# A chained down projection: order of low halves and sums in its first chunk, order and PSUM tiles in its last

## The chip, the cores and the metric

The kernel runs on one core of one Trainium2 chip. The metric is the device time of one execution in microseconds (us), lower is better. The core has a matrix engine (TensorE, PE in the profile), three engines for elementwise work (VectorE or DVE, ScalarE or ACT, GpSimd or POOL), a sync engine (SP) that issues DMAs, an on-chip memory (SBUF) of 128 partitions, and a small accumulator memory (PSUM) into which the matrix engine writes.

## The reference

One decoder layer on 1024 tokens of width 1024 in float32: norm, two gated branches, output projection and residual, then an MLP and a last norm. The change lies in the MLP's second product and the last norm:

```python
    h = rms_norm(x, g_mlp[l])
    f = jnp.square(jax.nn.relu(jnp.einsum("bsd,df->bsf", h, w_1[l])))
    x = x + jnp.einsum("bsf,fd->bsd", f, w_2[l])
return rms_norm(x, g_final)
```

Here f has 4096 columns, w_2 is 4096 x 1024, and rms_norm divides each token's row by the root of its mean square (plus 1e-6) and multiplies it by a gain per column. All of it is float32.

## The kernel before

**The down projection** (f times w_2) is the last stage. The 4096 rows of the sum are taken in four chunks (`g` = 0 to 3), each of two halves (`kk`) of 512 rows. In a chunk the output is cut into 2 x 2 blocks of 512 tokens by 512 columns and made by Winograd's form of Strassen's method: seven products (`p` = 1 to 7) instead of eight, at the price of sums of blocks before them and after them. Each product is float32 work on a matrix engine that here takes a reduced format (`float32r`), so each operand is split in two: a high half `h` (a copy into the format, by ScalarE) and a low half `l` (the rest). A product is then three matmuls: high by high, low by high, high by low.

**A step** is one (`g`, `p`, `kk`) of the list `dseq`: 24 matmuls of 128 x 128 by 128 x 512. `down_mm` does its first twelve for tokens 0 to 255 of the block (`q2` = 0), then twelve for the other 256 (`q2` = 1). The order of the products is 1, 2, 6, 5, 7, 3, 4; in the last chunk (`g` = 3) it is 1, 2, 6, 5, 3, 7, 4. Steps of a chunk are numbered `m` = 0 to 13.

**Operands.** Names in the profile: `da` are operand tiles of the left side (from f), `db` of the right side (from w_2), then product, half and h or l: `da_60l` is the low half of product 6, first half. `left_high` and `right` make the high half on ScalarE (one step or two ahead) and return a function that makes the low half on VectorE (`low`, L1176: source minus high). The other way to the low half is `by_dma` / `split_dma`: ScalarE writes minus the high half (L65), GpSimd issues a DMA that adds the source into it (L66), ScalarE writes the high half (L67); this takes nothing of VectorE's time. `d_sum` makes the sums of blocks on VectorE: `t1` to `t4` on the right side, `s1` to `s4` on the left. The tables `SUMS` (chunks 0 to 2) and `LAST` (chunk 3) say after which step each is made.

**Results.** `DBANK` says which PSUM tile a product goes to: a (products 1 and 2), b (6, 7, 4), e (5 and 3), two tiles of 128 x 1024 for the two `q2`. Products that share a tile are chained: product 3 goes on adding to what product 5 left in tile e. So between them `down_add` must have added the tile into the running output `acc` (L1970, VectorE), and the first matmul of product 3 into that tile has to wait for it. For `q2` = 1 this addition is held back to the start of the next step (`held`).

**Order.** VectorE, ScalarE and the matrix engine run strictly in the order in which this code issues instructions (a manual schedule). In a step the code issues: the held addition, the high half of the next step's left operand, the first sum due, the high half of a right operand two steps ahead, the first twelve matmuls, the addition for `q2` = 0, the low halves, the other sums, the residual's addition, the second twelve matmuls. In the last chunk `FX` hangs further work behind steps: operands by DMA and pieces of the last norm.

**The end.** Product 4 of the last chunk is not chained. `d_last` adds tile b and `acc` into fresh PSUM tiles f, and the four tiles of product 4 (tokens 512 to 1023, left 512 columns; 12 matmuls each) are accumulated onto them by `d_group`. Before, f0 and f1 were the two halves of one tile of 128 x 1024, f2 and f3 had a tile each. Tokens 0 to 511 are complete before that; `out_sq`, `out_root` and `out_scaled` do their norm (squares on ScalarE, root and its refinement on both, scaling on both) and issue their output DMAs. `close(n)` does the same for tokens 512 + 128 n and onwards: a square of f with a sum along the row (ScalarE), a root (ScalarE), six small instructions on VectorE that refine 1/root, then the scaling of the two halves and the output DMA. `out_pre` multiplies by the gain in advance.

Of the kernel before, what the change touches and what calls it, by code (L numbers as in the profile page):

```python
# [12 lines left out]
AF = mybir.ActivationFunctionType  # L13
# [4 lines left out]
D = 1024  # L18
HS = 512
# [11 lines left out]
def trunk_kernel(ctx: ExitStack, tc: tile.TileContext, x, xt_in, xt_eo, vecs, w_in, w_a_out, w_b_pl, w_b_sq,  # L31
# [1954 lines left out]
    LAST = {0: ("t1",), 1: ("t2", "s1"), 2: ("s2",), 4: ("s4",), 6: ("t3",), 7: ("s3",), 8: ("t4",)}  # L1986
# [45 lines left out]
    def d_last(q2):  # L2032

        b, a = du["b", q2], acc[1, 0, q2]
        if q2 == 0:
            f = unit("f0")
            tt(f, b, a, ALU.add)
            du["f", 0], du["f", 1] = (f[:, h] for h in HALVES)
        else:
            for q, h in enumerate(HALVES):  # L2040
                du["f", 2 + q] = f = unit(f"f{2 + q}")[:, 0:HS]
                tt(f, b[:, h], a[:, h], ALU.add)
        down_add(NC_ - 1, 7, q2)

    def close(n):
        t, (lo, hi) = 4 + n, HALVES
        ps, (q2, q) = du["f", n], divmod(n, 2)
        sa, sb, v, s, u, r = (sts[1, q2][:, i, q:q + 1] for i in range(6))
        nc.vector.tensor_scalar(sb, sb, 1.0 / D, EPS, ALU.mult, ALU.add)
        nc.scalar.activation(ro[t][:, lo], ps, AF.Square, accum_out=sa)  # L2050
        nc.scalar.activation(s, sa, AF.Sqrt, scale=1.0 / D, bias=sb)
# [4 lines left out]
        nc.vector.scalar_tensor_tensor(ro[t][:, lo], ps, r, gfin[:, lo], ALU.mult, ALU.mult)  # L2056
        if not q2:
            nc.vector.scalar_tensor_tensor(ro[t][:, hi], acc[1, 1, 0][:, HALVES[q]], r, gfin[:, hi],
                                           ALU.mult, ALU.mult)
        if n < 3:  # L2060
            nc.sync.dma_start(rows(t), ro[t])
        else:
            nc.sync.dma_start(rows(t)[:, lo], ro[t][:, lo])
            nc.scalar.dma_start(rows(t)[:, hi], ro[t][:, hi])

    def last_begun():
# [3 lines left out]
        for r in range(2):  # L2070
# [4 lines left out]
    FX = {2: ((last_begun,),), 4: ((out_sq, 0, 0, 0),), 5: ((out_sq, 0, 0, 1), (out_pre, 0, 0, 0)), 7: ((out_pre, 0, 0, 1),),  # L2075
          9: ((by_dma, "a", z, 7, 1), (by_dma, "b", z, 4, 0), (by_dma, "a", z, 4, 0), (out_sq, 0, 1, 0)),
          10: ((by_dma, "b", z, 4, 1), (by_dma, "a", z, 4, 1), (out_root, 0), (out_sq, 0, 1, 1), (out_scaled, 0))}
    held, xbs = None, {}
    with tc.manual_schedule(engines={mybir.EngineType.Activation, mybir.EngineType.DVE,
                                     mybir.EngineType.PE}):  # L2080
        for n, (g, p, kk) in enumerate(dseq[:-2]):
# [30 lines left out]
            for x in sums_:  # L2112
                d_sum(*x)
# [23 lines left out]

# [74 lines left out]
```

## Time and profile before

| | us |
|---|---|
| median of 3 runs (1540.29 to 1542.43) | 1540.67 |
| the profiled execution's own time | 1541.44 |
| its span, first to last instruction and transfer | 1539.6 |
| matrix engine busy | 1523.6 (99%) |
| VectorE busy | 1218.0 (79%) |
| ScalarE busy | 909.9 (59%) |
| down projection, first matmul to last | 1220.8 to 1528.8 |

The profile is of one execution. Times in it count from the span's start. A row of the timeline gives start, duration, engine, line, operation, tile written and tiles read, number of instructions, and in brackets how long the engine sat idle before and on whom it waited. Matmuls follow each other faster than one takes, since they are pipelined; the same holds to a smaller part for VectorE and ScalarE, so the step from one start to the next is what a queue of them costs.

### The profile page before, as it was taken

How to read it: one execution, taken by the hardware profiler on the slowest of the kernel's cores; microseconds unless marked ns; L12 is line 12 of the kernel's file. 1: busy time of each engine (PE TensorE's matmuls, PEld its weight loads, DVE VectorE, ACT ScalarE, POOL GpSimd, SP SyncE). 2: the span in 40 equal slices, each digit the busy share in tenths (PEclk: the TensorE clock that was granted, in tenths of full speed). 3: DMA queues.
4: the chain of work that ended last, by engine and by line, in shares of the span. 5: the costliest groups of instructions: out<-in, count | busy, mean ns of one | idle time of the engine just before them, and what ended most of it. 6: DMA issues, size and time to landing. Idle time of an engine off the chain costs nothing.

```text
span 1539.6 us, 19032 instructions
## 1 busy us (share of the span) xinstructions
PE 1523.6 (99%) x6734; PEld 1253.0 (81%) x6734; DVE 1218.0 (79%) x1647; ACT 909.9 (59%) x1272; POOL 169.2 (11%) x204
## 2 busy tenths in 40 slices
PE   9999999999999999999999999999999999999997
PEld 7888888888888888888888888888888888888875
DVE  6899999979899998788868879755555387777676
ACT  6648576657667566645575777544444454545465
POOL 0000000002222222000022322000000000101011
PEclk9999999999999999999999999999999999999999
DMA  8776978898998789963779898333333965767346
GB/s 347 197 190 158 251 188 217 220 264 226 245 254 204 193 192 249 309 225 121 268 198 304 180 209 199 133 135 111 111 110 116 318 222 137 197 172 206 67 83 178
DMA packets 132433, 304.16 MB, mean 198 GB/s; under 512 B 13248, under 2 KB 35264, under 8 KB 132336
## 3 DMA queue, kind: packets, MB, share of 16 engines
q1 hardware_dynamic: 104048, 234.79, 46.2%
q0 software_dynamic: 28144, 67.88, 24.1%
q8 instruction: 53, 0.87, 0.2%
q14 instruction: 44, 0.36, 0.1%
q10 hardware_dynamic: 144, 0.26, 0.0%
HBM read 149.79 MB, written 60.82 MB: 137 GB/s over the span
## 4 chain that ended last, share of the span: by engine, by line
PE 89%; issue 5%; DMA 3%; DVE 2%; POOL 1%; ACT 1%; SPq 0%; POOLq 0%; DVEq 0%; ACTq 0%
PE z L726 15%; PE d0b L1952 2%; PE d2b L1952 2%; PE d1b L1952 2%; PE z L258 2%; PE d0e L1952 1%; PE d3b L1952 1%; PE d3a L1952 1%; PE d2e L1952 1%; PE d2a L1952 1%; PE d1e L1952 1%; PE d1a L1952 1%; PE d3e L1952 1%; DMA win_raw<-in_w_in_dram 1%; PE rg L534 1%
## 5 line engine op out<-in xcount | busy, mean ns | idle before, releaser
L726 PE MATMUL z<-xh,win_h 128*128 128x512 f32 x400 | 124.9, 390 | 0.0
L726 PE MATMUL z<-xl,win_h 128*128 128x512 f32 x400 | 124.5, 389 | 0.0
L726 PE MATMUL z<-xh,win_l 128*128 128x512 f32 x400 | 98.4, 391 | 0.6 <-DMA win_l<-win_raw 0.6
L726 PEld LDWEIGHTS z<-xh,win_l 128*128 128x128 f32 x400 | 75.0, 188 | 17.9 <-DMA win_l<-win_raw 1.1
L726 PEld LDWEIGHTS z<-xh,win_h 128*128 128x128 f32 x400 | 75.0, 188 | 16.8 <-ACT win_h L67 0.7
L637 DVE SCALAR_TENSOR_TENSOR y<-u,vec,y 128x511 f32<-128x511 f32 (+14 forms) x120 | 88.3, 736 | 0.0
L726 PEld LDWEIGHTS z<-xl,win_h 128*128 128x128 f32 x400 | 75.1, 188 | 15.8
L542 ACT ACTIVATE g<-rg,vec 96x1024 f32<-96x1024 f32 x32 | 35.6, 1113 | 85.7 <-issue 46.0
L637 DVE SCALAR_TENSOR_TENSOR yt<-u,vec,yt 128x511 f32<-128x511 f32 (+6 forms) x112 | 82.5, 737 | 0.0
L637 DVE SCALAR_TENSOR_TENSOR y<-yt,csum,y 128x511 f32<-128x511 f32 (+6 forms) x112 | 82.5, 737 | 0.0
L1648 ACT ACTIVATE o<-s 128x512 fp32r<-128x512 f32 x56 | 33.7, 623 | 45.7 <-DVE s L1632 26.4
L66 POOL DMA_DIRECT2D win_l<-win_raw x25 | 21.5, 859 | 325.8 <-ACT win_l L65 313.5
L486 DVE SCALAR_TENSOR_TENSOR v<-xb,vec,v 128x1023 f32<-128x1023 f32 (+2 forms) x36 | 46.2, 1283 | 7.0 <-ACT v L477 6.1
L66 POOL DMA_DIRECT2D zo<-zw x42 | 36.2, 861 | 128.5 <-ACT zo L65 111.9
L66 POOL DMA_DIRECT2D db_10l<-br x4 | 3.4, 860 | 340.1 <-DMA br<-in_w_dram 254.1
L65 ACT ACTIVATE zo<-zw 128x512 fp32r<-128x512 f32 x42 | 26.3, 626 | 20.7 <-PE z9f L914 2.1
L1176 DVE TENSOR_TENSOR o<-s,o 128x512 fp32r<-128x512 f32 x56 | 37.3, 683 | 1.4 <-ACT o L1648 1.4
L66 POOL DMA_DIRECT2D zo<-zs x28 | 24.2, 863 | 77.2 <-ACT zo L65 71.9
L578 DVE TENSOR_TENSOR_SCAN g<-a,g 128x1024 f32<-128x1024 f32 x12 | 27.5, 2292 | 0.4
L67 ACT ACTIVATE win_h<-win_raw 128x1024 fp32r<-128x1024 f32 x25 | 26.1, 1046 | 0.0
L65 ACT ACTIVATE win_l<-win_raw 128x1024 fp32r<-128x1024 f32 x25 | 26.1, 1045 | 0.0
L67 ACT ACTIVATE zo<-zw 128x512 fp32r<-128x512 f32 x42 | 26.1, 621 | 0.0
(3122 smaller groups left out, 4829.9 us busy)
## 6 DMA issues: line engine op xcount, KB each, us to landing
w_raw<-in_w_dram SPq DMA_DIRECT2D x34, 512.0 KB, 5.5
br<-in_w_dram SPq DMA_DIRECT2D x32, 512.0 KB, 5.9
ar<-fd SPq DMA_DIRECT2D x32, 512.0 KB, 6.6
zw<-in_w_in_dram SPq DMA_DIRECT2D x28, 512.0 KB, 6.4
win_raw<-in_w_in_dram SPq DMA_DIRECT2D x25, 512.0 KB, 6.6
win_l<-win_raw POOLq DMA_DIRECT2D x25, 512.0 KB, 7.2
zo<-zw POOLq DMA_DIRECT2D x42, 256.0 KB, 5.7
gates<-zg SPq DMA_DIRECT2D x32, 256.0 KB, 4.1
```

The costliest lines, as they stand in the source:

```text
L65: nc.scalar.activation(l, src, AF.Copy, scale=-1.0)
L66: nc.gpsimd.dma_start(l, src, accum_op=ALU.add)
L67: nc.scalar.activation(h, src, AF.Copy)
L258: nc.tensor.matmul(z0[i][:, HALVES[hf]], w0[i][w][:, k, :], xpart(a, hf, k), start=k == 0 and which == "hh", stop=k == 7 and which == ("hl ...
L486: nc.vector.scalar_tensor_tensor(v[:, d:S], a[:, 0:S - d], cbw_c[:, w * 12 + t:w * 12 + t + 1], v[:, d:S], ALU.mult, ALU.add)
L542: nc.scalar.activation(a, gps.pop((n, gi))[:HD, :], AF.Sigmoid, bias=(ba_c, bx_c)[gi][:, n:n + 1])
L578: nc.vector.tensor_tensor_scan(i, a, i, 0.0, ALU.mult, ALU.add)
L637: nc.vector.scalar_tensor_tensor(o[:, k:], a[:, 0:HS - k], c, o[:, k:], ALU.mult, add)
L726: nc.tensor.matmul(zps[s][:, HALVES[hf]], w[:, k, :], xw[k][part][hf], start=n == 0, stop=n == 23)
L1176: tt(l, src, h.bitcast(F32), ALU.subtract)
L1648: nc.scalar.activation(o[:, 0], src, AF.Copy)
L1952: nc.tensor.matmul(o, a, b, start=start and n == 0, stop=stop and n == len(todo) - 1, skip_group_check=not start or not stop)
```

## The change

Three parts. First, in chunk 0 at steps 2 and 3 (`joint`) VectorE makes the low halves ahead of the sums, the sums in reversed order, and the addition of a finished tile behind both; before, one sum went first, and addition, low halves and other sums followed.

Second, in the last chunk: `t3` and `s3` are made earlier and no longer at once before product 3; the right operand of product 3's second half is split by DMA; product 4's left operands are split at steps 5 and 6 instead of 9 and 10, product 7's second left operand at step 8 instead of 9; `out_pre` for `q2` = 1 comes at step 6 and for `q2` = 0 at step 8 (5 and 7 before, in the other order); the roots and scalings of tokens 0 to 511 are all issued by the end of step 10 (those of tokens 256 to 511 stood behind the first of the four last tiles before).

Third, the end: each of f0, f1, f2 has a PSUM tile of its own, f3 is written over the second half of product 7's tile, and `close` is cut in two, of which the second half (`closed`) is issued one tile later.

```diff
     def right(g, p, kk):
-        if (p == 1 if g == 0 else not kk or p in (2, 5)):
+        if (p == 1 if g == 0 else not kk or p in (2, 5) or (g, p) == (NC_ - 1, 3)):
             by_dma("b", g, p, kk)
...
-    LAST = {0: ("t1",), 1: ("t2", "s1"), 2: ("s2",), 4: ("s4",), 6: ("t3",), 7: ("s3",), 8: ("t4",)}
+    LAST = {0: ("t1",), 1: ("t2", "s1"), 2: ("s2",), 4: ("s4", "t3"), 6: ("s3",), 8: ("t4",)}
...
         b, a = du["b", q2], acc[1, 0, q2]
-        if q2 == 0:
-            f = unit("f0")
-            tt(f, b, a, ALU.add)
-            du["f", 0], du["f", 1] = (f[:, h] for h in HALVES)
-        else:
-            for q, h in enumerate(HALVES):
-                du["f", 2 + q] = f = unit(f"f{2 + q}")[:, 0:HS]
-                tt(f, b[:, h], a[:, h], ALU.add)
-        down_add(NC_ - 1, 7, q2)
+        if q2:
+            down_add(NC_ - 1, 7, 1)
+        for q, h in enumerate(HALVES):
+            f = b[:, h] if q2 and q else unit(f"f{2 * q2 + q}")[:, 0:HS]
+            tt(f, b[:, h], a[:, h], ALU.add)
+            du["f", 2 * q2 + q] = f
+        if not q2:
+            down_add(NC_ - 1, 7, 0)
 
     def close(n):
+        t, lo = 4 + n, HALVES[0]
+        sa, sb, s = (sts[1, n // 2][:, i, n % 2:n % 2 + 1] for i in (0, 1, 3))
+        nc.vector.tensor_scalar(sb, sb, 1.0 / D, EPS, ALU.mult, ALU.add)
+        nc.scalar.activation(ro[t][:, lo], du["f", n], AF.Square, accum_out=sa)
+        nc.scalar.activation(s, sa, AF.Sqrt, scale=1.0 / D, bias=sb)
+
+    def closed(n):
         t, (lo, hi) = 4 + n, HALVES
...
-    FX = {2: ((last_begun,),), 4: ((out_sq, 0, 0, 0),), 5: ((out_sq, 0, 0, 1), (out_pre, 0, 0, 0)), 7: ((out_pre, 0, 0, 1),),
-          9: ((by_dma, "a", z, 7, 1), (by_dma, "b", z, 4, 0), (by_dma, "a", z, 4, 0), (out_sq, 0, 1, 0)),
-          10: ((by_dma, "b", z, 4, 1), (by_dma, "a", z, 4, 1), (out_root, 0), (out_sq, 0, 1, 1), (out_scaled, 0))}
+    FX = {2: ((last_begun,),), 4: ((out_sq, 0, 0, 0),), 5: ((by_dma, "a", z, 4, 0), (out_sq, 0, 0, 1)),
+          6: ((by_dma, "a", z, 4, 1), (out_pre, 0, 0, 1)), 8: ((by_dma, "a", z, 7, 1), (out_pre, 0, 0, 0)),
+          9: ((by_dma, "b", z, 4, 0), (out_sq, 0, 1, 0), (out_root, 0)),
+          10: ((by_dma, "b", z, 4, 1), (out_sq, 0, 1, 1), (out_scaled, 0), (out_root, 1), (out_scaled, 1))}
...
             sums_ = d_sums(g, m)
-            if sums_:
+            joint = not g and m in (2, 3)
+            if sums_ and not joint:
                 d_sum(*sums_.pop(0))
...
             down_mm(g, p, kk, 0)
+            if joint:
+                for f in lows_:
+                    f()
+                for x in sums_[::-1]:
+                    d_sum(*x)
             if kk:
...
-            for f in lows_:
-                f()
-            for x in sums_:
-                d_sum(*x)
+            if not joint:
+                for f in lows_:
+                    f()
+                for x in sums_:
+                    d_sum(*x)
...
         d_group(du["f", 0], z, 4, 0, (0, 1), False, True)
         d_last(1)
-        out_root(1)
         out_sq(1, 1, 0)
-        out_scaled(1)
         out_sq(1, 1, 1)
         out_pre(1, 1, 1)
+        close(0)
         d_group(du["f", 1], z, 4, P, (0, 1), False, True)
-        close(0)
+        closed(0)
+        close(1)
         d_group(du["f", 2], z, 4, 2 * P, (0, 1), False, True)
-        close(1)
+        closed(1)
+        close(2)
         d_group(du["f", 3], z, 4, 3 * P, (0, 1), False, True)
-        close(2)
         close(3)
+        closed(2)
+        closed(3)
```

**VectorE in chunk 0, steps 2 and 3** (product 2's second half and product 6's first): `t_0`, `t_1` are the sums t2 of the two halves kk, the rows of L1840 the sums s1, those of L1842 the sums s2, and `xb` takes the first finished tile. Before, from the second t on:

```order
L1850 TENSOR_TENSOR t_1_10343<-br_22_10194,br_11_10073 128x1024
L1176 TENSOR_TENSOR da_21l<-ar_12_10258,da_21h 128x1024
L1176 TENSOR_TENSOR db_60l<-t_0_10322,db_60h 128x1024
L1840 TENSOR_TENSOR s_1_10362<-ar_21_10196,ar_22_10256 128x1024
L1842 TENSOR_TENSOR s_0_10364<-s_0_10324,ar_11_10071 128x1024
L1842 TENSOR_TENSOR s_1_10381<-s_1_10362,ar_11_10075 128x1024
L1970 TENSOR_TENSOR xb_0_10260<-xb_0_10260,d0a_10271 128x1024
L1176 TENSOR_TENSOR da_60l<-s_0_10364,da_60h 128x1024
L1176 TENSOR_TENSOR db_61l<-t_1_10343,db_61h 128x1024
```

The change, the same stretch:

```order
L1176 TENSOR_TENSOR da_21l<-ar_12_10258,da_21h 128x1024
L1176 TENSOR_TENSOR db_60l<-t_0_10322,db_60h 128x1024
L1842 TENSOR_TENSOR s_0_10360<-s_0_10324,ar_11_10071 128x1024
L1840 TENSOR_TENSOR s_1_10362<-ar_21_10196,ar_22_10256 128x1024
L1850 TENSOR_TENSOR t_1_10364<-br_22_10194,br_11_10073 128x1024
L1176 TENSOR_TENSOR da_60l<-s_0_10360,da_60h 128x1024
L1176 TENSOR_TENSOR db_61l<-t_1_10364,db_61h 128x1024
L1842 TENSOR_TENSOR s_1_10398<-s_1_10362,ar_11_10075 128x1024
L1970 TENSOR_TENSOR xb_0_10260<-xb_0_10260,d0a_10271 128x1024
```

`da_60l` moves from the eighth place of this stretch to the sixth; s2 of the second half and the addition into xb go behind it.

**VectorE in the last chunk, around product 5's end and product 3's start**: the two rows of L1970 are the additions of tile e, for `q2` = 0 and 1. Before:

```order
L1970 TENSOR_TENSOR acc_10549<-acc_10549,d3e_12121 128x1024
L1176 TENSOR_TENSOR da_30l<-ar_12_11795,da_30h 128x1024
L1176 TENSOR_TENSOR db_31l<-br_22_11831,db_31h 128x1024
L1844 TENSOR_TENSOR ar_11_11563<-ar_11_11563,ar_21_11757 128x1024
L2010 TENSOR_TENSOR out_12105<-xb_1_10262,gfin 128x512
L2010 TENSOR_TENSOR out_12107<-xb_1_10262,gfin 128x512
L1970 TENSOR_TENSOR acc_10567<-acc_10567,d3e_12135 128x1024
```

The change:

```order
L1844 TENSOR_TENSOR ar_11_11641<-ar_11_11641,ar_21_11833 128x1024
L1970 TENSOR_TENSOR acc_10549<-acc_10549,d3e_12126 128x1024
L1176 TENSOR_TENSOR da_30l<-ar_12_11795,da_30h 128x1024
L1970 TENSOR_TENSOR acc_10567<-acc_10567,d3e_12140 128x1024
L1854 TENSOR_TENSOR br_21_11680<-br_21_11680,t_6_11933 128x1024
```

Of the four rows between the low half and the second addition none is left: one is now a DMA, the others stand earlier.

**VectorE at the end**, from the addition of product 7's last tile (`d3b`) to the first `close`: f rows are additions into the f tiles, `st_last` rows the small instructions of the norms. Before, with f2 and f3 (L2042) just ahead of this stretch and the first `close` (L2049) just behind it:

```order
L1970 TENSOR_TENSOR acc_10567<-acc_10567,d3b_11949 128x1024
L2014 TENSOR_TENSOR st_last_11993<-st_last_11993 128x2
L2015 TENSOR_SCALAR st_last_11993<-st_last_11993 128x2
L98 RECIPROCAL st_last_11993<-st_last_11993 128x2
L102 TENSOR_TENSOR st_last_11993<-st_last_11993 128x2
L103 TENSOR_TENSOR st_last_11993<-st_last_11993 128x2
L104 TENSOR_SCALAR st_last_11993<-st_last_11993 128x2
L105 TENSOR_TENSOR st_last_11993<-st_last_11993 128x2
L2028 SCALAR_TENSOR_TENSOR out_12105<-acc_10489,st_last_11993,gfin 128x512
L2028 SCALAR_TENSOR_TENSOR out_12107<-acc_10489,st_last_11993,gfin 128x512
L2010 TENSOR_TENSOR out_12385<-acc_10567,gfin 128x512
L2010 TENSOR_TENSOR out_12387<-acc_10567,gfin 128x512
```

The change:

```order
L1970 TENSOR_TENSOR acc_10567<-acc_10567,d3b_11949 128x1024
L2039 TENSOR_TENSOR f_12380<-d3b_11949,acc_10797 128x512
L2039 TENSOR_TENSOR d3b_11949<-d3b_11949,acc_10797 128x512
L2010 TENSOR_TENSOR out_12387<-acc_10567,gfin 128x512
L2010 TENSOR_TENSOR out_12389<-acc_10567,gfin 128x512
L2047 TENSOR_SCALAR st_last_11994<-st_last_11994 128x1
```

The norm of tokens 256 to 511 (`st_last_11993`, L2014 to L2028) no longer stands between product 7's last tile and the first `close`; it now stands ahead of the additions into f0 and f1.

More of the change, by code (lines that the diff above doesn't have):

```diff
@@ L2034, in d_last @@
         b, a = du["b", q2], acc[1, 0, q2]
[L2035 to L2045 removed]
+        if q2:
[6 more added lines that the diff above has]
+            down_add(NC_ - 1, 7, 0)
+    def close(n):
+        t, lo = 4 + n, HALVES[0]
[4 more added lines that the diff above has]
+    def closed(n):
         t, (lo, hi) = 4 + n, HALVES
[L2047 removed]
+        q2, q = divmod(n, 2)
         sa, sb, v, s, u, r = (sts[1, q2][:, i, q:q + 1] for i in range(6))
[L2049 to L2051 removed]
         nc.vector.scalar_tensor_tensor(v, sa, 1.0 / D, sb, ALU.mult, ALU.add)
@@ L2055, in close @@
             nc.scalar.activation(ro[t][:, hi], ro[t][:, hi], AF.Copy, scale=r)
-        nc.vector.scalar_tensor_tensor(ro[t][:, lo], ps, r, gfin[:, lo], ALU.mult, ALU.mult)
+        nc.vector.scalar_tensor_tensor(ro[t][:, lo], du["f", n], r, gfin[:, lo], ALU.mult, ALU.mult)
         if not q2:
```

## The prediction

> **What bounds the kernel now.** First the chain of work that ended last, by engine; then the busy time by window at the program's end (columns: window, length, busy time and count of the matrix engine PE, its weight loads, DVE, ACT and POOL, granted clock, DMA share, GB/s).
>
> ```profile
> PE 89%; issue 5%; DMA 3%; DVE 2%; POOL 1%; ACT 1%; SPq 0%; POOLq 0%; DVEq 0%; ACTq 0%
> ```
>
> ```profile
> 1499.30:1517.70 18.40, 18.40 (x82) 15.20 (x81) 13.18 (x19) 13.37 (x21) 4.28 (x5) 1.00 0.76 142
> 1528.80:1535.40 6.60, 0.00 (x0) 0.00 (x0) 5.22 (x19) 2.89 (x8) 0.00 (x0) 0.85 0.59 240
> 1535.40:1539.60 4.20, 0.00 (x0) 0.00 (x0) 0.00 (x0) 0.00 (x0) 0.00 (x0) 0.50 0.34 127
> ```
>
> The matrix engine is the bound nearly everywhere, so what VectorE and ScalarE do costs nothing except where the matrix engine waits for it, or after its last matmul. That last part is 10.8 us: 6.6 of elementwise work, 4.2 from the last DMA's issue to the end. Next the matrix engine's timeline in the down projection, where it waits twice, and the chain's row for one undisturbed product step pair (start, length, 48 matmuls):
>
> ```profile
> 1254.75 10.88 PE d0e L1952 x48
> ```
>
> ```profile
> 1242.59 0.39 PE L1952 MATMUL d0b<-db_60h,da_60h 128*128 128x512 f32 x1
> 1243.78 0.50 PE L1952 MATMUL d0b<-db_60h,da_60l 128*128 128x512 f32 x1 [0.80 <-DVE da_60l L1176]
> ...
> 1249.38 0.39 PE L1952 MATMUL d0b<-db_61h,da_61l 128*128 128x512 f32 x1
> ...
> 1496.31 0.61 PE L1952 MATMUL d3e<-db_30l,da_30h 128*128 128x512 f32 x2
> 1498.55 0.50 PE L1952 MATMUL d3e<-db_30h,da_30h 128*128 128x512 f32 x1 [1.62 <-DVE acc L1970]
> ...
> 1528.16 0.61 PE L1952 MATMUL f<-db_41l,da_41h 128*128 128x512 f32 x2
> ```
>
> A matmul follows the last one after 10.88 / 48 = 0.227 us. The first wait: the second matmul of product 6 was due at 1242.59 + 0.227 = 1242.82 and starts at 1243.78, 0.96 late; from there 24 intervals to 1249.38 take 5.60 instead of 5.44, so restarting costs 0.16 more. Stall one is worth 1.12. The second: due at 1496.31 + 2 x 0.227 = 1496.76, started at 1498.55, 1.79 late, with the same 0.15 for the restart 1.94. The last matmul ends at 1528.16 + 0.61 = 1528.77. The change touches exactly these two stalls and the end.
>
> **Part one, chunk 0.** VectorE's rows there:
>
> ```profile
> 1232.29 1.22 DVE L1850 TENSOR_TENSOR t<-br,br 128x1024 f32<-128x1024 f32 x1
> ...
> 1247.04 1.22 DVE L1176 TENSOR_TENSOR da_61l<-s,da_61h 128x1024 fp32r<-128x1024 f32 x1
> ```
>
> From the first to the last are thirteen places without a pause: 14.75 / 13 = 1.135 us each. The sum t is the first place, da_60l the tenth, so it started at 1242.51 and ended 1.22 later, where the matrix engine was let go. In the new order it has the eighth place from the same start: 1232.29 + 7 x 1.135 = 1240.24, done at 1241.46, 1.3 before it is due. The wait is gone. What is late next: da_61l, the fourteenth place in both orders, because only instructions ahead of it changed places. It still ends at 1247.04 + 1.22 = 1248.26. Without stall the matrix engine wants it at 1242.59 + 25 x 0.227 = 1248.26: a dead heat. VectorE may lose a little more, because the sum t of the second half now ends only at 1240.3, ScalarE's high half of it needs about 1.1 after that (twice the 0.58 of a 512-wide row further down), and db_61l has its turn at 1241.37. I charge 0.1 for a short wait there and 0.1 for its restart: the gain is 1.12 - 0.2 = 0.9. Bounds: 1.12 if the heat is won, 0.5 if da_61l comes 0.4 late. ScalarE's later rows slip with the sums by some 1.5 us, under the low halves of product 5, due five microseconds on.
>
> **Part two, last chunk.** VectorE's rows between the two additions of tile e:
>
> ```profile
> 1491.53 1.22 DVE L1970 TENSOR_TENSOR acc<-acc,d3e 128x1024 f32<-128x1024 f32 x1 [2.78 <-PE d3e L1952]
> 1492.66 1.22 DVE L1176 TENSOR_TENSOR da_30l<-ar,da_30h 128x1024 fp32r<-128x1024 f32 x1
> 1493.80 1.22 DVE L1176 TENSOR_TENSOR db_31l<-br,db_31h 128x1024 fp32r<-128x1024 f32 x1
> 1494.94 1.22 DVE L1844 TENSOR_TENSOR ar<-ar,ar 128x1024 f32<-128x1024 f32 x1
> 1496.07 1.29 DVE L2010 TENSOR_TENSOR out<-xb,gfin 128x512 f32<-128x512 f32 x2
> 1497.28 1.21 DVE L1970 TENSOR_TENSOR acc<-acc,d3e 128x1024 f32<-128x1024 f32 x1
> ```
>
> Four instructions, 1493.80 to 1497.28, stand before the addition that the matrix engine waits for. All four are gone from there. The addition then starts when its tile is complete (product 5's last matmul starts 13 intervals before 1496.76 and takes 0.39, so 1494.2) and ends near 1495.4, 1.3 ahead of need. Gain 1.94; I keep nothing back. What pays: the sums and the two multiplications by the gain move into gaps of VectorE such as the 2.78 us that it sat idle before the first of these rows. The low half db_31l becomes one more ScalarE write of about 1.1 and one more DMA. The rows for such DMAs and for the output:
>
> ```profile
> out_dram<-out SPq DMA_DIRECT2D x7, 512.0 KB, 3.1
> ...
> da_40l<-ar POOLq DMA_DIRECT2D x1, 512.0 KB, 6.4
> ...
> out_dram<-out SPq DMA_DIRECT2D x1, 256.0 KB, 2.6
> ```
>
> On GpSimd's queue the order is now da_40l, db_30l, da_41l, db_31l, db_70l, da_71l, db_40l, db_41l: two that stood at the end go ahead of four others. db_31l is read by the fifth matmul of its step, and `right` issues it two steps ahead: 2 x 5.44 + 4 x 0.227 = 11.8 us from the start of that step's matmuls, against 1.1 for ScalarE's write, 0.9 for GpSimd's issue and 6.4 to landing, 8.4 together. Covered, cost 0; uncovered it is the rival below.
>
> **Part three, the end.** VectorE, ScalarE, and the last DMA's issue:
>
> ```profile
> 1517.93 1.30 DVE L2042 TENSOR_TENSOR f<-d3b,acc 128x512 f32<-128x512 f32 x2 [0.37 <-PE d3b L1952]
> 1519.14 1.21 DVE L1970 TENSOR_TENSOR acc<-acc,d3b 128x1024 f32<-128x1024 f32 x1
> ...
> 1525.19 0.15 DVE L2049 TENSOR_SCALAR st_last<-st_last 128x1 f32<-128x1 f32 x1
> ...
> 1527.98 0.14 DVE L2049 TENSOR_SCALAR st_last<-st_last 128x1 f32<-128x1 f32 x1
> ```
>
> ```profile
> 1524.45 0.58 ACT L2050 ACTIVATE out<-f 128x512 f32<-128x512 f32 x1
> ...
> 1532.73 0.58 ACT L2050 ACTIVATE out<-f 128x512 f32<-128x512 f32 x1
> ```
>
> ```profile
> 1535.37 0.33 SPq L2063 DMA_DIRECT2D out_dram<-out  x1
> ```
>
> The last f tile is complete at 1528.77, but ScalarE squares it at 1532.73: 3.96 us lost to a backlog. From that square to the last issue are 2.64 (1532.73 to 1535.37), a chain of dependent small steps that the change keeps. The backlog's source: the first f tile was done by about 1520.6 (35 intervals before 1528.16, plus 0.39), its `close` began at 1525.19 on VectorE, and each `close` takes 2.79 (1525.19 to 1527.98), a shade more than a tile's 12 x 0.227 = 2.72, so the delay is never caught up. The 4.9 us between 1520.27 (1519.14 + 1.135) and 1525.19 are the norm of tokens 256 to 511 and two gain multiplications. The first part moves ahead, under product 7's matmuls, where its inputs exist and VectorE was busy 13.2 of 18.4 us (the window from 1499.3).
>
> New times, counted with the old matrix engine's clock: tile b complete at 1517.9, where VectorE's first row above starts; addition 1.14, two f additions 1.21, a semaphore step 0.1, two gain multiplications 1.21 (1496.07 to 1497.28): first `close` at 1521.6 instead of 1525.19. Two full closes of 2.79 bring 1527.2. The third, tokens 768 to 895, has one scaling on VectorE, not two: 2.79 less about 0.6, plus 0.1 for one more small instruction, so VectorE is free near 1529.5. The last square, now issued on ScalarE ahead of the third's scaling, starts at 1528.81 and with its row sum takes about 0.7: VectorE is wanted at 1529.5. It just fits. So the last issue comes at 1528.81 + 2.64 = 1531.45, not 1535.37: 3.9 gained. Bounds: 4.0 at most (the chain cannot start before the tile); 3.2 if the closes lose 0.7, as a queue that just fits may.
>
> Given back: the third output DMA now leaves about 0.9 us before the last two instead of 2.4, so 512 KB are in flight beside the last 512 KB. Alone the last lands 2.6 after issue. Lower bound 0; upper bound: the third lands 3.1 after its issue, 2.2 after the last issue, and only then 512 KB move at the window's 240 GB/s, 2.2 us: 4.4 against 2.6, or 1.8. I take 0.3, near the lower end, as both run on all DMA engines and only the remainder of the third is in the way.
>
> The Trainium skill, page "DMA: Bandwidth & Descriptors", section "Anatomy of one DMA — SWDGE (gpsimd) path", gives a transfer about 2.0 us plus its bytes over 436 GB/s, and the section "Issuing engines are not separate DMA queues" says that transfers from all engines share the same 16 DMA engines. For 256 KB that is an estimated 2.6, as the trace has it. By it the last 1 MB would end an estimated 4.4 us after the third's issue, 3.5 after the last: 0.9 given back instead of 0.3, and a time of 1534.8 instead of 1534.2.
>
> **The sum.** Span 1539.6 - 0.9 - 1.94 - 3.9 + 0.3 = 1533.2, less 6.4. The profiled execution took 1541.44 by its own time and the median of the runs is 1540.67; the same 6.4 off the median gives **1534.2**. Its own range is 1533.6 to 1535.7, from gains of 1.12 + 1.94 + 4.0 = 7.1 at best to 0.5 + 1.94 + 3.2 - 0.7 = 4.9.
>
> **Rivals.**
>
> *The first stall only moves.* da_61l has the same place as before, so if the new wait on ScalarE's copies grows, product 6's second half waits as long as its first did. For it: the dead heat. Against it: only 0.05 to 0.1 is seen to be lost. 1535.1.
>
> *The last transfers pile up.* The upper bound above, 1.8 instead of 0.3: 1535.7. For it: 1 MB in about a microsecond. Against: before, pairs of such outputs left close together as well.
>
> *The backlog stays.* Another link of the closing chain, say each close growing to three microseconds and more by waiting on ScalarE's square of the next tile, keeps the end as late after the last matmul as now. Only the stalls count: 1540.67 - 2.84 = 1537.8. Against it: three of four closes need nothing that is late.
>
> *GpSimd's DMAs become the bound: slower.* If the eight splitting DMAs were served one after another, each taking the 6.4 that da_40l took from issue to landing, they would need 8 x 6.4 = 51 us from about 1478.5 (step 5, where the first is issued, begins 3 x 5.44 before step 8's 1494.0), and db_41l would land near 1529.7, while the matrix engine, 2.8 early, wants it at 1517.2 (36 intervals before 1528.16, less 2.8): 12.5 us late, 1534.2 + 12.5 = 1546.7. It decides once they do not overlap, or one takes more than about 10 us to land. Against it: the issues
>
> ```profile
> 1506.81 0.86 POOL L66 DMA_DIRECT2D da_40l<-ar  x1 [1.05 <-DVE da_70l L1176]
> 1509.93 0.86 POOL L66 DMA_DIRECT2D db_41l<-br  x1 [2.27 <-ACT db_41l L65]
> ```
>
> are 3.1 apart where the first takes 6.4 to land: they overlap, and the new ones are spread wider.
>
> *The change does not reach the path*: another operand turns out as late as the one removed, at each of the places. 1540.7.
>
> **Chances.** Forecast 0.70, first stall moves 0.10, pile-up 0.06, backlog stays 0.07, DMAs bound 0.04, nothing 0.03. About 0.2% (3.1 us) is what a measurement here tells from no change, so faster means below 1537.6: 0.70 + 0.10 + 0.06 = 0.86; same 0.07 + 0.03 = 0.10; slower 0.04. The range 1533.0 to 1536.8 holds the first three cases; below 1533.6 it allows the 0.4 by which the fastest run shown lies under the median, and above it the larger bound for the last DMAs together with the smaller gains, 0.5 + 1.94 + 3.2 - 1.8 = 3.8.
>
> **What would show it.** In the changed kernel's profile: no wait of the matrix engine on da_60l, at most 0.3 on da_61l; no wait of d3e on acc; ScalarE's square of the last f tile within 0.1 of the last matmul's end; the last output DMA issued about 2.6 after it; a span near 1533.2. I am wrong if the matrix engine shows a new wait above half a microsecond in the last chunk, if VectorE still closes the third tile when the last square is done, or if landing takes over 3.5 after the last issue.

## The result, and the profile after

| | before | changed |
|---|---|---|
| median of 6 runs each, us | 1540.48 (1540.13 to 1542.43) | 1534.39 (1533.99 to 1534.71) |
| the profiled execution's own time | 1541.44 | 1534.40 |
| its span | 1539.6 | 1532.6 |

The changed kernel takes 0.9958 of the time before (95% interval 0.9946 to 0.9971): 6.1 us faster. The forecast was 1534.2, from 6.4 us gained.

The reader should set the two profiles side by side at fixed points of the matrix engine's stream, not by time from the start, since a shift that arose early goes through to the end. No matmul ahead of the one that opens product 2 in chunk 0 depends on a changed instruction. It and VectorE's row beside it, first of the kernel before, then of the changed one (timelines):

```profile
1231.15 1.23 DVE L1176 TENSOR_TENSOR db_21l<-br,db_21h 128x1024 fp32r<-128x1024 f32 x1 [1.18 <-DMA fd<-fb]
...
1231.71 0.39 PE L1952 MATMUL d0a<-db_20h,da_20h 128*128 128x512 f32 x1
```

```profile
1230.37 1.23 DVE L1176 TENSOR_TENSOR db_21l<-br,db_21h 128x1024 fp32r<-128x1024 f32 x1 [1.22 <-DMA fd<-fb]
...
1230.65 0.39 PE L1952 MATMUL d0a<-db_20h,da_20h 128*128 128x512 f32 x1
```

The changed kernel is already 1.06 us ahead here, in code that is the same in both. That belongs to these two executions and not to the change. VectorE's row is let go by a DMA (its bracket), so it need not shift with the matrix engine: its lead is 0.56 before and 0.28 now. From this point on the spans differ as follows (us):

| stretch | before | changed | gain | forecast |
|---|---|---|---|---|
| start to product 2 in chunk 0 | 1231.71 | 1230.65 | 1.06 | none |
| product 2 to product 5 in chunk 0 (first d0e; products 2 and 6) | 22.88 | 22.33 | 0.55 | 0.9 |
| to product 5 in the last chunk (first d3e) | 228.58 | 228.61 | -0.03 | 0 |
| product 5 to product 7 (both halves of products 5 and 3) | 23.69 | 21.76 | 1.93 | 1.94 |
| product 7 to the last matmul's end | 21.92 | 21.92 | 0 | 0 |
| last matmul's end to SP's last issue | 6.60 | 2.70 | 3.90 | 3.9 |
| last issue to the end of the span | 4.20 | 4.67 | -0.47 | -0.3 |

Without the first row the change is worth 5.9 us of span. Next the changed kernel's profile where the prediction looked. In the matrix engine's timeline one wait is left in the down projection, and no row of d3e has one:

```profile
1241.53 0.39 PE L1952 MATMUL d0b<-db_60h,da_60h 128*128 128x512 f32 x1
...
1247.62 0.50 PE L1952 MATMUL d0b<-db_61h,da_61l 128*128 128x512 f32 x1 [0.26 <-DVE da_61l L1176]
...
1495.18 0.39 PE L1952 MATMUL d3e<-db_30h,da_30h 128*128 128x512 f32 x1
...
1524.65 0.61 PE L1952 MATMUL d3b<-db_41l,da_41h 128*128 128x512 f32 x2
```

VectorE, where it lets the matrix engine go in chunk 0, in the last chunk, and at the three closes that it begins ahead of the last square:

```profile
1239.46 1.22 DVE L1176 TENSOR_TENSOR da_60l<-s,da_60h 128x1024 fp32r<-128x1024 f32 x1
1240.67 1.22 DVE L1176 TENSOR_TENSOR db_61l<-t,db_61h 128x1024 fp32r<-128x1024 f32 x1
...
1246.34 1.22 DVE L1176 TENSOR_TENSOR da_61l<-s,da_61h 128x1024 fp32r<-128x1024 f32 x1
...
1491.08 1.22 DVE L1176 TENSOR_TENSOR da_30l<-ar,da_30h 128x1024 fp32r<-128x1024 f32 x1
1492.67 1.22 DVE L1970 TENSOR_TENSOR acc<-acc,d3e 128x1024 f32<-128x1024 f32 x1 [0.36 <-PE d3e L1952]
...
1518.10 0.15 DVE L2047 TENSOR_SCALAR st_last<-st_last 128x1 f32<-128x1 f32 x1
...
1520.84 0.15 DVE L2047 TENSOR_SCALAR st_last<-st_last 128x1 f32<-128x1 f32 x1
...
1523.57 0.21 DVE L2047 TENSOR_SCALAR st_last<-st_last 128x1 f32<-128x1 f32 x2
...
1526.02 0.16 DVE L2055 SCALAR_TENSOR_TENSOR st_last<-st_last 128x1 f32<-128x1 f32 x1 [0.30 <-ACT out L2048]
```

The second addition into `acc` ends at 1493.89, and its reader starts at 1495.18: 1.3 to spare. The closes come 2.74 and 2.73 apart, no faster than the matrix engine makes tiles (2.72), and VectorE even idles 0.30 at the last. Then the last square on ScalarE, SP's last issue, the way of the output to memory, and three of GpSimd's eight splitting DMAs (queue, number, size, median us from issue to landing):

```profile
1525.30 0.60 ACT L2048 ACTIVATE out<-d3b 128x512 f32<-128x512 f32 x1 [1.20 <-PE d3b L1952]
```

```profile
1527.97 0.33 SPq L2066 DMA_DIRECT2D out_dram<-out  x1
```

```profile
da_40l<-ar POOLq DMA_DIRECT2D x1, 512.0 KB, 4.5
...
db_31l<-br POOLq DMA_DIRECT2D x1, 512.0 KB, 5.5
db_70l<-br POOLq DMA_DIRECT2D x1, 512.0 KB, 6.3
...
out_dram<-out ACTq DMA_DIRECT2D x1, 256.0 KB, 3.3
out_dram<-out SPq DMA_DIRECT2D x1, 256.0 KB, 3.0
```

The last square starts 0.04 after the last matmul ends (1524.65 + 0.61 = 1525.26). Before, it was 3.96.

### The profile page after: what moved, and what is told of

Read it like the earlier page. It is cut to its first block, busy times and chain, and to the rows that moved or that the text cites. A ratio compares the mean times of both kernels' runs of the same rounds, so it can differ in the third digit from the quotient of the medians.

```text
span 1532.6 us, 19039 instructions
## 1 busy us (share of the span) xinstructions
PE 1522.9 (99%) x6734; PEld 1252.9 (82%) x6734; DVE 1217.2 (79%) x1647; ACT 911.8 (59%) x1273; POOL 172.6 (11%) x205
## 4 chain that ended last, share of the span: by engine, by line
PE 91%; issue 4%; DMA 2%; POOL 1%; DVE 1%; ACT 0%; SPq 0%; POOLq 0%; DVEq 0%
PE z L726 18%; PE d1b L1952 2%; PE d2b L1952 2%; PE d0b L1952 2%; PE d3b L1952 2%; PE d0e L1952 1%; PE d3e L1952 1%; PE d3a L1952 1%; PE d2e L1952 1%; PE d2a L1952 1%; PE d1e L1952 1%; PE d1a L1952 1%; PE z L258 1%; PE rg L534 1%; PE rg L536 1%
```

## The experiments

Eleven runs follow, in three groups: ten new kernels and the changed kernel once more. In each group the kernel before ran again on the same chip (medians 1540.39, 1540.26 and 1540.18), and a ratio below is to its own group's median.

**One part alone.** Each of the first three kernels is the kernel before with one part of the change. `chunk0_only` has the `joint` order; `last_chunk_only` has `LAST`, `right` and `FX`, with the norm of tokens 256 to 511 left behind the first of the last tiles; `end_only` has the third part, with that norm in step 10. Against the kernel before, and cut to what tells them apart:

```diff
# chunk0_only
+            joint = not g and m in (2, 3)
# last_chunk_only
+    LAST = {0: ("t1",), 1: ("t2", "s1"), 2: ("s2",), 4: ("s4", "t3"), 6: ("s3",), 8: ("t4",)}
+          10: ((by_dma, "b", z, 4, 1), (out_sq, 0, 1, 1), (out_scaled, 0))}
# end_only
-          10: (..., (out_scaled, 0))}
+          10: (..., (out_scaled, 0), (out_root, 1), (out_scaled, 1))}
-        out_root(1)
-        out_scaled(1)
+        close(0)
```

The fourth, `norm_late`, is the changed kernel with one thing undone:

```diff
-          10: (..., (out_scaled, 0), (out_root, 1), (out_scaled, 1))}
+          10: (..., (out_scaled, 0))}
...
         d_last(1)
+        out_root(1)
         out_sq(1, 1, 0)
+        out_scaled(1)
```

> The kernel before with the first part of the change alone (chunk 0, steps 2 and 3: low halves ahead of sums and additions). Theory: the matrix engine's wait on da_60l (0.80 idle, 1.12 with the restart) goes, and a shorter wait on da_61l takes its place, as in the changed kernel's trace (0.26 idle), so 0.5 to 0.9 us of the 6.1 measured: 1539.6 to 1540.0. The last chunk keeps its wait of 1.6 on the addition of tile e, and the last DMA is still issued 6.6 after the last matmul ends. Rival (the stall only moves): da_61l waits as long as da_60l did, time unchanged at 1540.5 and an idle time of 0.7 or more on da_61l.

> The kernel before with the second part alone: sums t3 and s3 earlier, product 3's second right operand by DMA, left operands of product 4 earlier, gain multiplications moved; the norm of tokens 256 to 511, the f tiles and the closing stay as before. Theory: the wait of d3e on acc goes and nothing takes its place: 1.9 less, 1538.5; the wait on da_60l (0.8) stays, and the last DMA is issued 6.6 us after the last matmul ends as before, since the closing backlog does not depend on it. Rival (the closing backlog came from the splits and multiplications that stood late in the last chunk): the end shortens too, by a microsecond or more, 1537.5 or less.

> The kernel before with the third part alone: norm of tokens 256 to 511 issued by step 10, f tiles of their own, closing cut in two. Theory: both stalls stay (0.8 and 1.6), the last DMA is issued 2.7 to 3.1 after the last matmul's end instead of 6.6; VectorE, which has more to do ahead of the additions into f0 while the second part's moves are missing, may make the first of the four last tiles wait up to 1 us. 2.5 to 3.5 less: 1537.0 to 1538.0. Rival (the end needs the second part as well): the last DMA is issued 4 or more after the last matmul, less than 2 us gained.

> The changed kernel with one thing put back: the root and scaling of tokens 256 to 511 are issued behind the first of the four last tiles again. Theory (this norm is what delays the closing): the first close starts about 3 us later on VectorE and is not caught up, because a close takes 2.73 and a tile 2.72; the last DMA is issued 5.3 to 5.6 after the last matmul instead of 2.7, the time is 2.5 to 2.9 longer than the changed kernel's 1534.4: 1536.9 to 1537.3. Rival (the cut of close in two, or the f tiles of their own, brought the gain): the last DMA is still issued within 3.2 of the last matmul, 1534.4 to 1534.9.

| | median (range), us | ratio to before | chunk 0 | product 5 to 7 | product 7 to last matmul's end | to last issue |
|---|---|---|---|---|---|---|
| chunk0_only | 1539.65 (1539.14 to 1540.49) | 0.9996 [0.9987, 1.0005] | 22.27 | 23.67 | 21.92 | 6.61 |
| last_chunk_only | 1538.43 (1538.03 to 1539.12) | 0.9989 [0.9979, 0.9998] | 22.81 | 21.76 | 21.92 | 6.62 |
| end_only | 1537.97 (1537.53 to 1539.60) | 0.9985 [0.9975, 0.9994] | 22.73 | 23.71 | 22.99 | 3.23 |
| norm_late | 1537.21 (1536.56 to 1537.88) | 0.9979 [0.9970, 0.9988] | 21.82 | 21.76 | 21.92 | 5.76 |

("chunk 0" is the stretch from product 2 to product 5 of the table further up.) All four times lie where they were expected. Two ends are a little later than expected: 5.76 in `norm_late` (5.3 to 5.6) and 3.23 in `end_only` (2.7 to 3.1). The interval of `chunk0_only` contains 1, so its median alone would not tell it from the kernel before; its stretch in chunk 0 does. Each part moves its own stretch and, but for one, no other (why 22.73 to 22.88 and 21.82 to 22.33 scatter in chunk 0 comes with the last group). The exception is `end_only`; its matrix engine waits (engine, tile, line, released by: us in total, times, longest):

```profile
PE d3e L1952 <- DVE acc L1970: 1.6, 1, 1.6
PE f L1952 <- DVE f L2039: 0.8, 1, 0.8
PE d0b L1952 <- DVE da_60l L1176: 0.7, 1, 0.7
```

and VectorE just ahead of the tile that the second row names:

```profile
1511.11 0.17 DVE L98 RECIPROCAL st_last<-st_last 128x2 f32<-128x2 f32 x1 [3.37 <-ACT st_last L2016]
...
1515.06 1.42 DVE L2028 SCALAR_TENSOR_TENSOR out<-acc,st_last,gfin 128x512 f32<-128x512 f32 x2
1516.39 1.29 DVE L2039 TENSOR_TENSOR f<-d3b,acc 128x512 f32<-128x512 f32 x2
```

Without the rest of the last chunk's new order the two norms of tokens 0 to 511 both stand in front of the f tiles. The first holds VectorE 3.37 us, because ScalarE makes its root only behind the splits of product 4's second half, and the matrix engine waits 0.83 for the f tiles. So the end depends on the second part: the three parts alone bring 0.7, 2.0 and 2.4 off the median, 5.1 together, and in one kernel 6.1.

`norm_late` says that the norm's place is worth 5.76 - 2.70 = 3.06 of the 3.90, given the rest. What the rest is worth without it was the next question.

**Tiles and close.** `close_whole` is the changed kernel with the close in one piece, behind the next tile:

```diff
-        close(0)
         d_group(du["f", 1], z, 4, P, (0, 1), False, True)
+        close(0)
         closed(0)
-        close(1)
         d_group(du["f", 2], z, 4, 2 * P, (0, 1), False, True)
+        close(1)
         closed(1)
-        close(2)
         d_group(du["f", 3], z, 4, 3 * P, (0, 1), False, True)
-        close(3)
+        close(2)
         closed(2)
+        close(3)
         closed(3)
```

`f01_one_tile` is the changed kernel with `d_last` as before: f0 and f1 are halves of one PSUM tile again, f3 has a tile of its own, and for `q2` = 1 the addition into `acc` comes behind those into the f tiles again instead of ahead of them.

```diff
+        if q2 == 0:
+            f = unit("f0")
+            tt(f, b, a, ALU.add)
+            du["f", 0], du["f", 1] = (f[:, h] for h in HALVES)
...
```

`f01_one_tile_whole_close` has both edits, so that of the third part only the early norm is left.

> The changed kernel, with the close of a last tile in one piece again and issued behind the next tile, as before the change; the tiles of PSUM of their own stay. Theory (the cut of the close only decides when an output leaves, since ScalarE's squares and TensorE wait for nothing that the close holds): TensorE shows the changed kernel's waits and no new one, the last matmul's end to the last DMA issue stays at 2.6 to 2.9 us (2.70 in the changed kernel), the output before the last is issued 2 to 2.6 us ahead of the last one instead of 1.0, so that the last landing is shorter by up to 0.5 us: 1533.8 to 1534.5. Rival (the cut was part of what cleared the backlog): end to last issue 3.2 us or more, 1534.9 or later.

> The changed kernel, with the first two of the four last tiles as halves of one PSUM tile of 128x1024 again, in the changed order of issue. Theory (the tile decides who waits for whom): ScalarE's square of the first half is issued ahead of the matmuls of the second, so those now wait until it has read the shared tile: a new wait of TensorE of 1.2 to 2.2 us behind the first of the last tiles, the end of the last matmul to the last issue at 2.6 to 2.9 us, time 1535.6 to 1536.8. Rival (the tiles don't matter; the early norm alone cleared the backlog): no wait of TensorE there, 1534.0 to 1534.8.

> The changed kernel, with the two last tiles in one PSUM tile and the close in one piece behind the next tile, both as before the change; only the early norm stays of the part on the end. Theory: no wait of TensorE, but ScalarE's square of the first half runs only behind the matmuls of the second (some 2.7 us later than in the changed kernel), the closes follow one another that much later, and the last matmul's end to the last issue is 3.2 to 5.0 us instead of 2.70: 1534.9 to 1536.7. Rival (the norm alone was the backlog): end to last issue 2.6 to 2.9 us and 1534.0 to 1534.8.

| norm | f0, f1 | close | kernel | last matmul's end to last issue | median (range), us |
|---|---|---|---|---|---|
| late | one tile | whole | before | 6.60 | 1540.48 (1540.13 to 1542.43) |
| late | own tiles | cut | norm_late | 5.76 | 1537.21 (1536.56 to 1537.88) |
| early | one tile | whole | f01_one_tile_whole_close | 5.28 | 1536.27 (1535.92 to 1537.26) |
| early | one tile | cut | f01_one_tile | 2.69, matmuls 2.0 longer | 1536.32 (1535.88 to 1537.44) |
| early | own tiles | whole | close_whole | 2.97 | 1533.84 (1533.56 to 1534.47) |
| early | own tiles | cut | changed | 2.70 | 1534.39 (1533.99 to 1534.71) |

All rows but the first also have the first two parts of the change, so the first row's time can't be set beside the others. Its end can, since `last_chunk_only` has 6.62 there. The early norm alone brings the end 6.60 - 5.28 = 1.3 nearer, the own tiles and the cut close alone 6.60 - 5.76 = 0.8, both together 3.9: two causes held the same square, and taking one away left the other. The second cause already stands in the kernel before, where ScalarE's square of f1 waits for VectorE's scaling of f0:

```profile
1527.43 0.60 ACT L2050 ACTIVATE out<-f 128x512 f32<-128x512 f32 x1 [1.71 <-DVE out L2056]
```

How the shared tile holds it stands in ScalarE's timeline of `f01_one_tile_whole_close`, below two rows of the matrix engine (the end of f0, then of f1):

```profile
1517.26 0.62 PE L1952 MATMUL f<-db_41l,da_41h 128*128 128x512 f32 x2
...
1519.98 0.62 PE L1952 MATMUL f<-db_41l,da_41h 128*128 128x512 f32 x2
```

```profile
1517.65 0.63 ACT L2005 ACTIVATE out<-acc 128x512 f32<-128x512 f32 x1 [1.45 <-DVE acc L1970]
...
1518.80 0.18 ACT L2005 ACTIVATION_READ_ACCUMULATOR out<-acc 128x1 f32 x1
...
1520.64 0.60 ACT L2049 ACTIVATE out<-f 128x512 f32<-128x512 f32 x1 [1.65 <-PE f L1952]
...
1523.37 0.60 ACT L2049 ACTIVATE out<-f 128x512 f32<-128x512 f32 x1 [1.72 <-DVE out L2060]
```

f0 is complete at 1517.26 + 0.62 = 1517.88 and ScalarE free at 1518.98, but the square of f0 starts when f1 is complete, at 1520.6; the square of f1 then waits until VectorE (L2060) has read f0 for its scaling. With the cut close the square is issued ahead of f1's matmuls, and it is the matrix engine that waits for it (ScalarE's row and the matrix engine's in `f01_one_tile`):

```profile
1518.03 0.57 ACT L2049 ACTIVATE out<-f 128x512 f32<-128x512 f32 x1
```

```profile
1518.75 0.50 PE L1952 MATMUL f<-db_40h,da_40h 128*128 128x512 f32 x1 [1.73 <-ACT out L2049]
```

So the halves of this tile are not free of each other in either order of issue; the order decides which engine pays. Not all of the price is the tile's. With `d_last` as before `acc` is complete later, so ScalarE's squares of the right 512 columns come later (its first row above waits for `acc`), and ScalarE is free only 1.1 us after f0 is complete, in both kernels about as late. In the one the tile's own share is the 1.65 that ScalarE then sits idle; in the other the tile is why the matrix engine waits at all, and some 1.0 of the 1.73 is ScalarE's lateness (f0 is complete at 1517.01 there). The tile and the order of additions were not run apart.

The cut itself did not clear the backlog. `close_whole` ends 0.27 later after the last matmul, since ScalarE does the third tile's scaling ahead of the last square, but its output before the last leaves 2.45 ahead of the last one, and the landing is back at 2.8:

```profile
out_dram<-out ACTq DMA_DIRECT2D x1, 256.0 KB, 2.8
out_dram<-out SPq DMA_DIRECT2D x1, 256.0 KB, 2.6
```

From SP's last issue to the span's end it takes 4.17, the changed kernel 4.67: 0.5 won for 0.27 lost. The time is where the theory had it, though its range overlaps the changed kernel's, so that it is faster is not shown; its 2.97 is just above the theory's 2.6 to 2.9 and far from what a backlog would show, as are the 5.28 of `f01_one_tile_whole_close` above its 3.2 to 5.0. The wait of 1.73 and both times with one tile are inside the expected ranges, and the rivals (the tiles don't matter; the norm alone was the backlog) fall.

**One low half back on VectorE.** `db31_on_vector` undoes the edit of `right`:

```diff
-        if (p == 1 if g == 0 else not kk or p in (2, 5) or (g, p) == (NC_ - 1, 3)):
+        if (p == 1 if g == 0 else not kk or p in (2, 5)):
```

> The changed kernel without the one low half that the change moved from VectorE to GpSimd's DMA in the last chunk (db_31l is VectorE's again). Theory (the new order of the last chunk alone takes the sum out of TensorE's way): the sum's second addition ends about 0.8 us later than in the changed kernel, where it was done 1.3 us ahead of its need, so TensorE shows no wait on the sum, and the time stays at 1534.0 to 1534.8. Rival (the move to the DMA was what cleared the stall): the wait of TensorE on the sum is back at 0.3 us or more, 1534.9 to 1536.3.

1534.50 us (1533.78 to 1534.97), no wait of the matrix engine, 21.76 from d3e to product 7. VectorE's second addition of tile e in this kernel:

```profile
1492.79 1.21 DVE L1970 TENSOR_TENSOR acc<-acc,d3e 128x1024 f32<-128x1024 f32 x1
```

It ends at 1494.0. The stream is 0.56 us earlier here than in the changed kernel, so its reader is due at 1495.18 - 0.56 = 1494.62: 0.6 to spare. The move of db_31l to a DMA was not needed for the time: with that low half back on VectorE, two instructions (da_30l and db_31l) instead of five stand between the two additions, since the sum and the two multiplications by the gain keep their new places. Whether taking away one of these three would have been enough was not run.

**Chunk 0.** Steps 2 and 3 are the two halves of product 2, in which VectorE makes, among others, the low halves for product 2's second half and product 6's first; step 4 is product 6's first half, in which da_61l is made. The last group has the changed kernel again, the changed kernel with the joint order at step 4 too, and with that and the whole close:

```diff
-            joint = not g and m in (2, 3)
+            joint = not g and m in (2, 3, 4)
```

> The changed kernel as it is, for its time beside the two kernels of this group and for a second profile of the place in chunk 0. Theory (the wait on da_61l in the profile of the changed kernel was as long as VectorE happened to be behind: it began db_21l 0.28 us ahead of TensorE's first matmul with db_20h, against 0.46 to 0.76 in four of the kernels run here): the stretch from that matmul to the first matmul of d0e is about 22.6 us less that lead, so 21.8 to 22.3, and the time 1533.9 to 1534.7. Rival (the wait is a fixed part of the new order): 22.33 again whatever the lead.

> The changed kernel with the joint order (low halves ahead of sums) at one more step, so that da_61l is made one sum (about 1.1 us) earlier and that sum later. Theory (da_61l is the last thing that TensorE waits for in chunk 0): the stretch from the first matmul with db_20h to the first of d0e falls to 21.8 us or less whatever the lead, and the time by 0.1 to 0.5 against the changed kernel of this group: 1533.7 to 1534.2. Rival (the sum that goes behind is late in its place): a new wait of TensorE or ScalarE there, and no gain or a loss up to 1.1: 1534.4 to 1535.5.

> The changed kernel with the joint order at one more step, and the close of a last tile in one piece behind the next tile (close_whole gave 1533.84 with that alone). Theory: the two gains lie in different places and add up: the stretch in chunk 0 at 21.8 or less, last matmul's end to last issue 2.97, last issue to the end of the span 4.17, time 1533.3 to 1533.9. Rival (the differences are within what executions scatter): 1534.2 to 1534.6.

| | order in chunk 0 | VectorE's lead at product 2 | product 2 to product 5 | median (range), us |
|---|---|---|---|---|
| before | old | 0.56 | 22.88 | 1540.18 (1539.79 to 1540.96) |
| last_chunk_only | old | 0.61 | 22.81 | |
| end_only | old | 0.69 | 22.73 | |
| changed, first profile | joint at 2, 3 | 0.28 | 22.33 | |
| chunk0_only | joint at 2, 3 | 0.33 | 22.27 | |
| f01_one_tile_whole_close | joint at 2, 3 | 0.46 | 22.13 | |
| after_again | joint at 2, 3 | 0.60 | 22.04 | 1534.22 (1534.09 to 1535.00) |
| db31_on_vector | joint at 2, 3 | 0.71 | 21.86 | |
| norm_late | joint at 2, 3 | 0.76 | 21.82 | |
| joint_steps_2_4 | joint at 2 to 4 | 0.40 | 21.76 | 1534.58 (1534.16 to 1535.00) |
| best | joint at 2 to 4 | 0.78 | 21.76 | 1534.01 (1533.38 to 1534.29) |

(The lead is how long before the matrix engine's first matmul with db_20h VectorE begins db_21l; stretches are of the one profile of each kernel, the before row's median is this group's.) In the old order lead and stretch add up to 23.4 in each row, with the joint order at steps 2 and 3 to 22.6, both within 0.04 (so do `close_whole`, 0.62 and 21.97, and `f01_one_tile`, 0.59 and 22.02): the wait is as long as VectorE happens to be behind, and at one and the same lead the joint order is worth 0.8. With step 4 as well the stretch is 21.76 at either lead, which is 96 matmuls at 0.227 without a gap, as product 5 to product 7 takes now. So da_61l was the last thing waited for. The time does not show it: `joint_steps_2_4` has 1534.58 against 1534.22 of the changed kernel in the same group. Its profile starts product 2 at 1231.34, the changed kernel's at 1230.69; the 0.65 come from ahead of the edit and outweigh the 0.28 gained. Neither the expected 1533.7 to 1534.2 nor a new wait was seen. `best` is at 1534.01, above the expected 1533.9 and by no more than 0.2 below its neighbour: the two fixes show in the stretches, but whether the kernel is faster for them stays open at this scatter.

## Why the prediction was right, point by point

- **Stall one.** That da_60l is let go, and that da_61l is next in a dead heat, came out. The size was off: 0.55 for 0.9. The mis-sized term is "I charge 0.1 for a short wait there and 0.1 for its restart". At the lead of the old profile, 0.56, the charge is 22.6 - 0.56 - 21.76 = 0.3, not 0.2, since db_61l did wait for ScalarE's copy by 0.075 (1239.46 to 1240.67 is 1.21, not 1.135; the copy, in the row below, ends at 1240.63). The other 0.28 is not of the change: the lead was 0.28 instead of 0.56 in this execution, and every bit of it is paid while da_61l is late. A dead heat should have been priced as a range over executions.

```profile
1239.57 1.06 ACT L1880 ACTIVATE db_61h<-t 128x1024 fp32r<-128x1024 f32 x1 [1.21 <-DVE t L1850]
```

- **Stall two.** 1.93 for 1.94, with 1.3 to spare as worked out. `last_chunk_only` shows it alone. The DMA for db_31l was covered (5.5 to landing), but the wait goes without it too.
- **The end.** 3.90 for 3.9: last square 0.04 after the last matmul, closes 2.74 apart, "it just fits" to 0.30. The size was right and the cause only in part. The prediction put the backlog's source down to the 4.9 us in front of the first close and did not price the PSUM tiles. Its new times took it for granted that ScalarE squares f0 when f0 is done; with f0 and f1 in one tile it does so only when f1 is done too, and the early norm alone is worth 1.3. It came out because the change makes both edits; as an account of the cause that is in part luck.
- **Given back.** 0.47 for 0.3. The prediction took the 2.6 of SP's output for the last landing. What lands last is ScalarE's output, issued beside it: 2.8 after issue before, 3.3 now. The output before the last is issued 1.01 ahead of the last one; at 1.53 (`norm_late`, landing 2.8) nothing is given back. So the term is a matter of that half microsecond. The Trainium skill, page "DMA: Bandwidth & Descriptors", section "Anatomy of one DMA — SWDGE (gpsimd) path" (2.0 us plus bytes over 436 GB/s, fitted to DMAs that GpSimd issues, while these leave by SP and ScalarE), with its section "Issuing engines are not separate DMA queues", would put the end of the last 1 MB at an estimated 4.4 - 1.01 = 3.4 after the last issue, where the trace has 3.3. For the last two alone, 512 KB, it would give an estimated 3.2, where the trace has 2.8. As a price of the change it did worse than the prediction's term: the prediction's estimate by that page was 0.9, its term 0.3, and 0.47 was measured.
- **The rivals.** "The first stall only moves" came true by half at most. Against a stretch without a gap, 21.76, the new wait costs 22.33 - 21.76 = 0.57 in the first profile of the changed kernel and 22.04 - 21.76 = 0.28 in the second, where the old one cost 1.12. (The bracket of 0.26 counts from the end of the matmul before. Undelayed, a matmul starts 0.16 ahead of that end, and the restart costs the other 0.15.) The pile-up of transfers is 0.2 beyond the term, not 1.5. The backlog did not stay. GpSimd's DMAs did not become the bound: the eight land 4.5 to 6.3 after issue and overlap, and no matmul waits for one. (That rival's own sum starts too late: 1494.0 - 3 x 5.44 is 1477.7, not 1478.5, so its price should have been 0.8 lower.)
- **The sum.** Of the 6.9 by which the spans differ, 1.06 are not the change's; what is left, 5.9, agrees with the medians (6.1). The forecast of 6.4 is 0.35 too high at stall one and 0.17 at the landing, and that is the whole difference. That the time came out only 0.2 from the forecast while the gain was 0.3 off is luck: the forecast was taken off 1540.67, the median of three runs, and the median of six is 1540.48.

## What to carry to other kernels

A late end can have two causes that hold the same instruction: undoing each alone (3.1 for the norm's place, with the rest in place) and doing each alone (1.3) give different prices, and only both tell that the parts need each other. Before a PSUM tile is shared by two results, look at who reads the first half while the second is written: with the order of additions that came with it, the shared tile cost 2.0 us of the matrix engine in one order of issue and 2.3 of closing time in the other. Where a producer and a consumer arrive together, read their distance in several executions, since a heat won in one is lost in the next.

## What the runs showed of the hardware

Executions of the same code differ ahead of the change by more than some of its terms are worth: the first matmul of product 2 started between 1230.3 and 1231.7 in thirteen profiles. The changed kernel was 1.12 us ahead of the kernel before already at 362 us (the first matmul into z0a, before and changed):

```profile
362.06 0.39 PE L914 MATMUL z0a<-xh,zo 128*128 128x512 f32 x1
```

```profile
360.94 0.39 PE L914 MATMUL z0a<-xh,zo 128*128 128x512 f32 x1
```

Ahead of that the kernel before has a wait in its list that the changed one has not:

```profile
PE z L726 <- DMA win_l<-win_raw: 0.6, 1, 0.6
```

The rest of the 1.12 was not traced further.

Two engines that read different halves of one PSUM tile were kept apart too: the square of f1 waited 1.72 for VectorE's reading of f0. Who releases a wait is read from semaphore events here, so this wait, and those of the matmuls and squares on the shared tile, show what the program's instructions were made to wait for. Whether the chip would have needed it was not tried.
